# Hybrid encoder layer: moving the bases of the two SBUF stacks from 96 to 0 modulo 128 bytes

## The chip, the cores and the metric

The program runs on one core of one Trainium2 chip, as one launch. The metric is the device time of that launch in microseconds. The kernel before took 2280.51 us, the median of three runs (2278.97, 2280.51 and 2280.64).

## The reference

One encoder layer is applied to two sequences (256 and 1,024 tokens, 1,024 channels, float32) with shared weights. In outline:

```
x = LN(alpha*x + mix(x) @ w_out)      # mix: one input projection, split between
                                      #   a two-way Mamba-2 SSD group (16 heads) and a two-way GLA group (4 heads)
x = LN(alpha*x + cross_attention(x, mem))   # 4 heads, 256 memory tokens a sequence
x = LN(alpha*x + square(relu(x @ w_ff1)) @ w_ff2)   # 4,096 hidden channels
```

All matrices are float32, and the result must keep close to float32 accuracy.

## The kernel before, in words

The 1,280 tokens are ten tiles of 128. Nearly every product is made of three matmuls in the type fp32r: an operand is parted into a rounded part and a remainder (ScalarE copies it into fp32r, VectorE subtracts), and high by high, high by low and low by high are summed in PSUM. A matmul has 512 or 256 columns as a rule and loads its own 128x128 weights. A few products run in plain float32, each as two matmul records, and TensorE also transposes by the identity matrix `ident`.

The work goes in stages: the channel-major input projection with the gates and the convolution (`ch_majors`, L152; `gates`, L365 to L390; `conv`, L463 and L465; `conv_end`, L471; `conv_transposed`, L486 and L487), the token-major projection (`tok_majors`, L167) beside the backward states (L211) and the decay masks, the SSD and GLA passes with the output projection (`project`, L770; `gla_att`, L849), cross-attention (L1024 to L1083), FF1 in a Strassen-like scheme (`prod`, L1222), and FF2 in the same scheme (`mms`, L1445). TensorE's order is written out by hand; SyncE issues nearly all DMAs in program order, each waiting for its own buffers.

What matters here is where tiles lie. SBUF is laid out by two stacks of pools, in bytes of a partition. The **left stack** begins after 1,024 bytes of DMA scratch, four constants of 32 bytes each, `ident` (512), `nhalf` (32) and `gmix` (64): its first further tile, `raw` of the pool `ring`, starts at 1,760, which is 32 modulo 64, 96 modulo 128 and 224 modulo 256. Above it lie the weights `w` of `ring` (9,952) and the stage pools (`p1`, `w5`, `pb`, `mx`, `q2`, `q3`, `pk`, `p4`, `p7`, `pab`, `pa`, `pacc`). The **right stack** grows downwards from 229,344 (96 modulo 128) with `sc`, `io`, `pm`, `px`, `pl` and `pb8`. Sizes are rounded up to 32 bytes, and nearly all of them are multiples of 128, so nearly all tiles of the left stack lie at 96 modulo 128. Right of them, `pm`, `px`, `pl` and `pb8` lie at 96 modulo 128 too, while `io` and parts of `pb` and `q3` lie at 32.

There is one place where residues are mixed. The tag `t5` of the pool `w5` (stage of L152) has eleven buffers of 1,284 floats, 5,136 bytes, which take 5,152: a multiple of 32 and not of 64. So consecutive `t5` buffers start at 0 and at 32 modulo 64 in turn, and all four residues modulo 128 occur. The tiles `xraw`, `gl`, `glg`, `gex`, `cacc`, `csil`, `cxt`, `q` and `k` are such buffers. Of `xraw`, the one for k = 3 starts at 158,304 (32 modulo 64, 96 modulo 256), and the one for k = 4 at 194,368 (0 modulo 64, 64 modulo 256). Two more tiles of `w5` start at 0 modulo 64 (64 modulo 128): `wgk` (143,936) and `lrT` (148,032), the weights and the moving operand of the gates' matmul at L365; and `ident` starts at 1,152, which is 0 modulo 128.

A tile in one stack can take bytes that a closed pool of the other stack held; its first writer then waits for the last reader of those bytes. The tile `X22h` of `pa` ends at 136,928, where `gb3` of `pb8` begins, and `oT` of `p7` ends at 116,448, where the second `hh` buffer of `pb8` begins. `pl` begins at 137,056, which is 128 bytes above the end of `pa`.

Of the kernel before, what the change touches and what calls it, by code (L numbers as in the profile page):

```python
# [8 lines left out]
F32 = mybir.dt.float32  # L9
# [8 lines left out]
P = 128  # L18
# [15 lines left out]
def encoder_layer(ctx: ExitStack, tc: tile.TileContext, A, out, hook=None):  # L34
# [4 lines left out]
    cst = ctx.enter_context(tc.tile_pool(name="cst", bufs=1))  # L39
# [44 lines left out]
        return e.enter_context(tc.tile_pool(name=name, bufs=bufs, reuse_waits="tile", side=side))  # L84

    gmix = cst.tile([P, 16], F32, name="gmix")

    def load_raw(src):
        raw = ring.tile([P, D], F32, tag="raw", name="raw", bufs=2)
        SP.dma_start(raw, src)  # L90
        return raw
# [1501 lines left out]
```

## Time and profile before

| | us |
|---|---|
| median of three runs | 2280.51 |
| lowest and highest run | 2278.97, 2280.64 |
| the profiled execution's own time | 2281.95 |
| its span, first to last instruction | 2280.2 |
| TensorE busy in it | 2243.9 (98%) |
| VectorE, ScalarE, GpSimd busy | 1445.1, 842.5, 353.2 |

The profile is one execution. Its span is what the views divide up; its own time has 1.75 us more around the span. A matmul's record lasts longer than the step from one matmul to the next, since they overlap: the step is the busy time of a long unbroken group divided by its count. The columns of DMA in the view of stretches are the mean share in which the 16 DMA engines were busy and what they moved.

### The profile page before, as it was taken

How to read it: one execution, taken by the hardware profiler on the slowest of the kernel's cores; microseconds unless marked ns; L12 is line 12 of the kernel's file. 1: busy time of each engine (PE TensorE's matmuls, PEld its weight loads, DVE VectorE, ACT ScalarE, POOL GpSimd, SP SyncE). 2: the span in 40 equal slices, each digit the busy share in tenths (PEclk: the TensorE clock that was granted, in tenths of full speed). 3: DMA queues.
4: the chain of work that ended last, by engine and by line, in shares of the span. 5: the costliest groups of instructions: out<-in, count | busy, mean ns of one | idle time of the engine just before them, and what ended most of it. 6: DMA issues, size and time to landing. Idle time of an engine off the chain costs nothing.

```text
span 2280.2 us, 28989 instructions
## 1 busy us (share of the span) xinstructions
PE 2243.9 (98%) x11532; PEld 1910.0 (84%) x11532; DVE 1445.1 (63%) x1760; ACT 842.5 (37%) x1326; POOL 353.2 (15%) x284
## 2 busy tenths in 40 slices
PE   9899999999998999999999999999999999999998
PEld 7788888888877888888888899888888887888887
DVE  5667765578967876898520266585655546675448
ACT  5464332243324324443421333254344434333331
POOL 2114000222223553343000011100000000000002
PEclk9999999999999999999999999999999999999999
DMA  5434326678777556653633432123433349754343
GB/s 177 114 121 129 95 79 218 223 245 275 270 265 267 203 194 245 241 185 130 198 119 85 171 120 83 66 96 128 156 120 135 142 153 332 271 177 139 93 146 140
DMA packets 164637, 384.49 MB, mean 169 GB/s; under 512 B 12899, under 2 KB 67107, under 8 KB 161942
## 3 DMA queue, kind: packets, MB, share of 16 engines
q1 hardware_dynamic: 136310, 363.51, 46.7%
q10 hardware_dynamic: 28192, 19.14, 2.7%
q8 instruction: 90, 1.47, 0.3%
q14 instruction: 45, 0.37, 0.0%
HBM read 262.83 MB, written 119.77 MB: 168 GB/s over the span
## 4 chain that ended last, share of the span: by engine, by line
PE 65%; DVE 3%; DMA 2%; issue 1%; ACT 1%; POOL 0%; POOLq 0%; DVEq 0%; ACTq 0%; SPq 0%
PE ps L1445 16%; PE ps L1222 13%; PE ps L770 8%; PE ps L152 7%; PE ps L1072 5%; PE ps L211 4%; PE ps L1232 4%; PE ps L167 3%; PE ps L1057 2%; DMA raw<-in_w_out 1%; PE ps L702 1%; PE ps L177 1%; PE ps L849 1%; DVE w L112 0%; PE ps L1045 0%
## 5 line engine op out<-in xcount | busy, mean ns | idle before, releaser
L1445 PE MATMUL ps<-w,hh 128*128 128x512 f32 x1608 | 364.9, 389 | 0.6 <-DVE w L1139 0.6
L1445 PEld LDWEIGHTS ps<-w,hh 128*128 128x128 f32 x1608 | 301.8, 188 | 63.6 <-DVE w L1139 1.1
L167 PE MATMUL ps<-w,xh 128*128 128x512 f32 x960 | 299.0, 393 | 2.3 <-DVE w L109 2.3
L152 PE MATMUL ps<-xh,w 128*128 128x512 f32 (+1 forms) x1008 | 232.2, 362 | 7.2 <-ACT k L424 5.3
L770 PE MATMUL ps<-w,mT 128*128 128x512 f32 x960 | 225.4, 393 | 4.5 <-DVE mT L182 2.4
L770 PEld LDWEIGHTS ps<-w,mT 128*128 128x128 f32 x960 | 179.7, 189 | 42.5 <-DVE mT L182 2.8
L167 PEld LDWEIGHTS ps<-w,xh 128*128 128x128 f32 x960 | 179.2, 188 | 39.8 <-DVE w L109 2.7
L152 PEld LDWEIGHTS ps<-xh,w 128*128 128x128 f32 x1008 | 169.1, 190 | 38.4 <-ACT k L424 5.7
L167 PE MATMUL ps<-w,xl 128*128 128x512 f32 x480 | 187.5, 391 | 0.0
L109 DVE TENSOR_TENSOR w<-raw,w 128x1024 fp32r<-128x1024 f32 x65 | 79.3, 1223 | 169.3 <-ACT w L108 169.0
L1362 DVE TENSOR_TENSOR hh<-hr,hh 128x1280 fp32r<-128x1280 f32 (+1 forms) x56 | 80.3, 1434 | 119.9 <-ACT hh L1361 119.9
L1361 ACT ACTIVATE hh<-hr 128x1280 fp32r<-128x1280 f32 (+1 forms) x56 | 68.8, 1228 | 192.4 <-PE ps L1445 180.4
L152 PE MATMUL ps<-xl,w 128*128 128x512 f32 (+1 forms) x504 | 127.5, 361 | 0.0
L1432 POOL TENSOR_SCALAR lnrs<-lnmv 128x1 f32<-128x1 f32 x10 | 5.4, 538 | 758.1 <-DVE lnmv L1430 758.1
L1072 PE MATMUL ps<-w,oT 128*128 128x512 f32 x480 | 110.8, 390 | 0.0
L108 ACT ACTIVATE w<-raw 128x1024 fp32r<-128x1024 f32 x81 | 86.2, 1066 | 63.6 <-PE ps L167 16.1
L671 POOL TENSOR_TENSOR row<-row,cb 128x1024 f32<-128x1024 f32 x20 | 52.8, 2652 | 354.9 <-ACT cb L655 229.2
L167 PEld LDWEIGHTS ps<-w,xl 128*128 128x128 f32 x480 | 90.3, 188 | 19.2
L1139 DVE TENSOR_TENSOR w<-raw,w 128x1024 fp32r<-128x1024 f32 x64 | 70.2, 1100 | 55.3 <-ACT w L1138 55.3
L1072 PEld LDWEIGHTS ps<-w,oT 128*128 128x128 f32 x480 | 89.5, 188 | 18.1
L152 PEld LDWEIGHTS ps<-xl,w 128*128 128x128 f32 x504 | 84.9, 190 | 15.0
L1232 PE MATMUL ps<-x,w 128*128 128x256 f32 x512 | 92.9, 280 | 0.0
(343 smaller groups left out, 4315.4 us busy)
## 6 DMA issues: line engine op xcount, KB each, us to landing
hr<-d_h SPq DMA_DIRECT2D x56, 640.0 KB, 3.9
row<-d_acs SPq DMA_DIRECT2D x40, 512.0 KB, 4.6
d_h<-a SPq DMA_DIRECT2D x16, 1280.0 KB, 4.5
raw<-in_w_ff SPq DMA_DIRECT2D x33, 512.0 KB, 3.5
w<-in_w_ff SPq DMA_DIRECT2D x32, 512.0 KB, 4.8
d_h<-V SPq DMA_DIRECT2D x16, 960.0 KB, 5.5
raw<-in_w_tok SPq DMA_DIRECT2D x28, 512.0 KB, 4.7
raw<-in_w_ch SPq DMA_DIRECT2D x21, 512.0 KB, 3.6
```

The lines of the kernel that those rows point to most:

```text
L108: ACT.activation(w[:, 0], raw, AF.Copy)
L109: eng.tensor_tensor(w[:, 1], raw, f32(w[:, 0]), op=ALU.subtract)
L152: PE.matmul(t[:, :n], wv[:, s, k, :], xx[k][:, o:o + n], start=(k == 0 and i == 0), stop=(k == KD - 1 and i == 2))
L167: PE.matmul(ps, xx[k][:, sl], wv[:, s, k % 2, :], start=(k == 0 and i == 0), stop=(k == KD - 1 and i == 2))
L211: PE.matmul(ps, a[:, p], b[:, q], start=start and i == 0, stop=stop and i == 2)
L770: PE.matmul(ps[j], mT[:, a, k, :], ws[k][:, s, j * 512:(j + 1) * 512], start=(k == 0 and i == 0), stop=(k == KD - 1 and i == 2))
L1072: PE.matmul(ps[j], oT[:, a, k, :], wm[k][:, s, j * 512:(j + 1) * 512], start=(k == 0 and i == 0), stop=(k == KD - 1 and i == 2))
L1139: DVE.tensor_tensor(w[:, 1], raw, f32(w[:, 0]), op=ALU.subtract)
L1222: PE.matmul(ps, wt[:, s, o + k * P:o + (k + 1) * P], xx[:, k, :], start=start and k == 0 and i == 0, stop=stop and k == 3 and i == 2, skip ...
L1232: PE.matmul(ps[:, j * 256:(j + 1) * 256], wt[:, s, o + k % 4 * P:o + (k % 4 + 1) * P], xe[x][:, k, :], start=k == 0 and i == 0, stop=k == ...
L1362: DVE.tensor_tensor(t[:, 1], raw, f32(t[:, 0]), op=ALU.subtract)
L1445: PE.matmul(ps, h[:, a, f, q * P:(q + 1) * P], w[:, b, f * 512:(f + 1) * 512], start=start and i == 0, stop=stop and i == 2, skip_group_ch ...
```

## The change

The pool `cst`, at the base of the left stack, gets a tile of 8 floats (32 bytes) behind `gmix`, and a new pool of one tile of 24 floats (96 bytes) is opened first on the right stack. Nothing reads or writes either tile. The list of instructions stays what it was, with other SBUF addresses: each tile of the left stack behind `gmix` lies 32 bytes higher (`raw` at 1,792 = 14 x 128), each tile of the right stack 96 bytes lower (its top at 229,248 = 1,791 x 128).

```
     gmix = cst.tile([P, 16], F32, name="gmix")
+
+    cst.tile([P, 8], F32, name="left_gap")
+    ctx.enter_context(tc.tile_pool(name="gap", bufs=1, side="right")).tile([P, 24], F32, name="right_gap")
```

## Rows read from the trace of the kernel before

**Rows 1.** From the profile's page: the span, the busy time of the engines, the clock granted to TensorE in 40 slices, and the shares of the chain that ended last.

```profile
span 2280.2 us, 28989 instructions
...
PE 2243.9 (98%) x11532; PEld 1910.0 (84%) x11532; DVE 1445.1 (63%) x1760; ACT 842.5 (37%) x1326; POOL 353.2 (15%) x284
...
PEclk9999999999999999999999999999999999999999
...
PE 65%; DVE 3%; DMA 2%; issue 1%; ACT 1%; POOL 0%; POOLq 0%; DVEq 0%; ACTq 0%; SPq 0%
```

**Rows 2.** The view of stretches, whole stages: start and end in us, its length, busy time and instructions of each engine, granted clock, busy share of the DMA engines and GB/s.

```profile
100.00:300.00 200.00, 200.00 (x1056) 170.03 (x1055) 136.53 (x104) 95.56 (x163) 39.75 (x32) 1.00 0.37 114
300.00:640.00 340.00, 337.43 (x1608) 282.08 (x1607) 242.66 (x291) 111.29 (x175) 66.00 (x26) 0.99 0.66 224
640.00:900.00 260.00, 250.36 (x1313) 211.38 (x1312) 190.00 (x272) 88.08 (x174) 107.19 (x82) 0.99 0.68 233
1890.00:2281.00 391.00, 381.40 (x1682) 315.26 (x1680) 244.32 (x240) 127.91 (x121) 14.91 (x20) 1.00 0.54 183
```

**Rows 3.** What TensorE's matmuls waited for, longest first in total: us, times, longest.

```profile
PE ps L152 <- ACT k L424: 5.3, 1, 5.3
PE ps L211 <- DVE ccp L205: 3.6, 1, 3.6
PE ps L211 <- DVE hl L205: 2.6, 3, 1.9
```

**Rows 4.** TensorE's matmuls in order of time around 136 us: start, length, line, tiles, the shape of the first, and the count. Each of the two rows is one run of 256, 512 and 512 columns.

```profile
135.49 0.75 PE L152 MATMUL ps<-xh,w 128*128 128x256 f32 x3
136.07 0.75 PE L365 MATMUL ps<-lrT,wgk 96*128 96x256 f32 x3
```

**Rows 5.** TensorE's weight loads at the same place, in order of time.

```profile
135.84 0.54 PEld L365 LDWEIGHTS ps<-lrT,wgk 96*128 96x128 f32 x3
136.42 0.54 PEld L152 LDWEIGHTS ps<-xh,w 128*128 128x128 f32 x3
```

**Rows 6.** The views of single lines whose tiles are `t5` buffers at mixed residues: count, shortest, median and longest duration in ns, start of the first and the last.

```profile
L486 PEld LDWEIGHTS ps<-ident,cacc x100: 138/140/146, 230.3 to 353.8; 128*128 128x128 f32 x100
L463 DVE TENSOR_SCALAR cacc<-ub,small x12: 942/945/970, 200.1 to 357.4; 128x1284 f32<-128x1284 f32 x12
L388 DVE SCALAR_TENSOR_TENSOR gex<-gex,k x8: 1479/1484/1487, 89.0 to 204.7; 128x1280 f32<-128x1280 f32 x8
L387 ACT ACTIVATE gex<-glg x16: 1254/1262/1278, 86.3 to 203.1; 128x1280 f32<-128x1280 f32 x16
L471 ACT ACTIVATE csil<-cacc x12: 1277/1314/1322, 214.5 to 366.1; 128x1284 f32<-128x1284 f32 x12
```

**Rows 7.** The view of stretches while the `xraw` tiles for k = 3 (first row) and k = 4 (second row) land; columns as in rows 2.

```profile
10.50:12.00 1.50, 1.50 (x6) 1.21 (x6) 0.97 (x1) 1.26 (x1) 0.00 (x0) 1.00 1.02 423
12.10:13.60 1.50, 1.50 (x6) 1.21 (x5) 1.44 (x1) 1.27 (x1) 0.00 (x0) 1.00 1.01 420
```

**Rows 8.** Groups of matmuls of 128 columns by line: count, busy us, mean ns of one, idle time before. The first has `ident` as the moving operand.

```profile
L486 PE MATMUL ps<-ident,cacc 128*128 128x128 f32 x100 | 12.4, 272 | 0.0
L849 PE MATMUL ps<-qk 128*128 128x128 f32 x160 | 19.5, 275 | 0.0
```

**Rows 9.** Matmuls of L211 in the stretch from 600 to 1060 us, as in rows 6. `gbp` and `qp` lie at the same residue modulo 128 (96), `gfp` (32) and `qp` (96) do not.

```profile
L211 PE MATMUL ps<-gbp,qp x96: 281/285/290, 890.5 to 1049.0; 128*128 128x256 f32 x96
L211 PE MATMUL ps<-gfp,qp x84: 278/279/283, 907.0 to 1048.6; 128*128 128x256 f32 x84
```

**Rows 10.** The matmul groups of FF2, as in rows 8.

```profile
L1445 PE MATMUL ps<-w,hh 128*128 128x512 f32 x1608 | 364.9, 389 | 0.6 <-DVE w L1139 0.6
...
L1445 PE MATMUL ps<-w,he 128*128 128x512 f32 x72 | 16.5, 389 | 0.0
```

**Rows 11.** The instructions that use `X22h` and `oT`, as in rows 6.

```profile
L1222 PE MATMUL ps<-X22h,w x128: 389/389/499, 1509.7 to 1889.9; 128*128 128x512 f32 x128
...
L1072 PE MATMUL ps<-w,oT x480: 389/389/476, 1312.4 to 1487.4; 128*128 128x512 f32 x160
```

**Rows 12.** In order of time: the load of `gb3` on SyncE's queue and the first write of `hh` after FF1's middle.

```profile
1952.85 0.43 SPq L1496 DMA_DIRECT2D gb<-in_ln  x1
...
1880.34 1.28 ACT L1361 ACTIVATE hh<-hr 128x1280 fp32r<-128x1280 f32 x1 [4.02 <-PE ps L1222]
```

## The prediction, made before the changed kernel ran

> **What bounds the kernel now.** [...] What is to be seen is that only 2280.2 - 2243.9 = 36.3 us of the span have no matmul in flight. The stretches [rows 2] say where: 9.6 us between 640 and 900, 9.6 in the last stage (which holds the final normalisation), 2.6 between 300 and 640, none between 100 and 300. TensorE's own waits [rows 3] are single events; the longest is 5.3 us. So two things could move the time: a matmul step that gets shorter or longer, which counts 11,532 times, or the few waits.
>
> **The change, part by part.** It adds no instruction and removes none, so no term of the sum is an instruction. Nor is a step moved past another one, and every queue, SyncE's and GpSimd's among them, keeps its order. What moves is the address of nearly every operand, by 32 bytes up in the left stack and 96 down in the right one. That can act in five ways.
>
> *1. Start of an operand modulo 64, TensorE.* The trace of before already has both cases side by side. At 135.49 us a run of 256, 512 and 512 columns has both operands at 32 modulo 64 (`xh`, `w`); at 136.07 a run of the same shape has both at 0 modulo 64 (`lrT`, `wgk`). Both take 0.75 us [rows 4], and three weight loads take 0.54 us in either [rows 5]. (The second has 96 rows in place of 128; the columns are the same.) Cost of the alignment: 0, within the 0.01 us in which the rows are written.
>
> *2. The same for the other engines.* Lines that work on `t5` buffers hop between 0 and 32 modulo 64 from one instruction to the next. Were the start to matter, each line would show two durations. The weight loads of L486, which meet all four residues modulo 128, go from 138 to 146 ns with the median at 140; VectorE's L463 and L388 have a median within 3 to 5 ns of their shortest; ScalarE's L387 and L471 spread by 24 and 45 ns of some 1,300 [rows 6]. No row gives GpSimd this test; its share of the chain is 0% [rows 1], so that I put it at 0 as well: VectorE and TensorE, which end the chain, are the cover, and if that were gone a few per cent of 353.2 us busy would be the price. Most of these instructions also run beside TensorE's matmuls, so that even the 45 ns would be hidden.
>
> *3. DMA.* The tile for k = 3, at 32 modulo 64, landed while all 16 engines were busy and moved 423 GB/s; the one for k = 4, at 0 modulo 64, 420 [rows 7]. That is 0.7%, and against the aligned one. DMA is 2% of the chain, 45.6 us, so the bound is 0.3 us to either side; I take 0. [...]
>
> *4. A start at 0 modulo 128, TensorE.* Here the trace of before has no fp32r matmul. The nearest rows are of 128 columns: the transposes move `ident`, which lies at 0 modulo 128, and last 272 ns; the plain products of L849 move operands at 32 modulo 128 and last 275 [rows 8]. If the 3 ns were the address, 11,532 of them are 34.6 us. The other end is a loss of the same 3 ns, for which no row speaks. I take 0: the two groups differ in kind as well (a transpose is one record of its own kind, a plain product two), and the weight loads in rows 6 did not care for 0 modulo 128. [...]
>
> *5. The stacks come 128 bytes closer.* Within a stack all distances stay. Between them they shift by 128, so in FF2 `w` (9,952) and `hh` (116,448), whose distance is now a multiple of 256, will be 128 off. For an effect of distance the nearest rows are L211's: with the same residue (`gbp`, `qp`) the median is 285 ns, with another (`gfp`, `qp`) 279 [rows 9]. FF2 has 1,608 + 72 = 1,680 such matmuls [rows 10]; at 6 ns that is 10.1 us, up or down, since which distance is the better is open. I take 0, because FF2's step of 364.9 us / 1,608 = 227 ns shows no room where the operands wait for each other.
>
> Closer stacks also make new overlaps in time. `gb3` now takes the last 128 bytes of `X22h`, so its load must wait for that tile's last reader, and on SyncE's queue the loads of `hr` and `w` would stand behind it, and TensorE behind those. But `X22h` is last read at 1889.9 us [rows 11] and the load goes out at 1952.85 [rows 12]: 63 us of slack, so 0. The second `hh` buffer now overlaps `oT`, last read by a matmul that begins at 1487.4 [rows 11], while `hh` is written from 1880.3 on [rows 12]: 0 too. The gap of 128 bytes below `pl` is used up exactly, so the tiles still fit.
>
> The sum is 0. Against the profiled execution, whose own time is 2281.95 us, that is 2281.95; the median of the runs shown is 1.44 lower, and for a median I predict **2280.5 us**.
>
> **The rivals.**
>
> *Faster: the fp32r matmul gains from 0 modulo 128.* Price 3 ns a matmul, 34.6 us, 2246. For it: rows 8. Against it: rows 4 and 6, in which halfway to that alignment, and for weight loads all the way, nothing changed. Chance 0.06.
>
> *Slower: the distance between the stacks.* The place is FF2, where `w` and `hh` lie in different stacks, the price 6 ns for each of 1,680 matmuls, 10.1 us, 2290.6. It decides if a distance that is an odd multiple of 128 is the bad one for two operands read at once. For it: in rows 9 the distance goes with 6 ns. Against it: there the equal residue is the slower one, and the two groups also stand at other places of their sequences. Chance 0.05.
>
> [...]
>
> *The change does not reach what it says.* In `io`, a tile goes from 32 to 64 modulo 128, and the `t5` buffers only swap residues. This holds whatever the effect is, and would shrink any of the above; the time stays at 2280.5.
>
> **How the numbers follow.** A measurement of this kernel can tell about 0.2%, 4.6 us, from no change. No change, with the 0.3 us of DMA and the 2.4 below it, has 0.87; the gain at 0 modulo 128 has 0.06, to which 0.01 comes for the distance turning out better (2270.4); the loss by distance 0.05, and 0.01 for a loss at 0 modulo 128. So faster 0.07, same 0.87, slower 0.06. As the case "same" holds more than 8 in 10 alone, the range is its own: below, 2280.5 - 2.4 and the 1.5 us by which the lowest run lies under the median, rounded to 2277; above, the same 3.5 us, 2284.
>
> **What would show it.** Right: FF2's group again at 227 ns a step, the 256-512-512 run at L152 again at 0.75 us, L463 at 945 ns and busy sums of all engines within 0.2%. The faster rival would show at once in L1445 and L167, records of 386 ns or less in place of 389, and a TensorE busy time near 2,210 us. The slower one would show in L1445 alone, with L167 and L770 unchanged. [...] The prediction is wrong if the median leaves 2277 to 2284, whichever step does it.

## The result, and the profile after

The changed kernel is slower: median 2299.74 us (four runs, 2296.55 to 2303.68) against 2280.57 (2278.97 to 2282.47), a ratio of 1.0088 with the interval 1.0076 to 1.0101, 17 to 23 us. The forecast of 2280.5 and its range of 2277 to 2284 are wrong. In the code after, every line behind the edit has a number higher by 3: L1445 is L1448.

The page of the changed kernel, its parts 1, 2 and 4, answers to [rows 1]. The profiled execution's own time is 2297.25 us.

```profile
span 2295.5 us, 28989 instructions
...
PE 2260.1 (98%) x11532; PEld 1910.1 (83%) x11532; DVE 1445.3 (63%) x1760; ACT 841.8 (37%) x1326; POOL 351.3 (15%) x284
...
PEclk9999999999999999999999999999999999999999
...
PE 66%; DVE 3%; DMA 2%; issue 1%; ACT 1%; POOL 1%; POOLq 0%; DVEq 0%; ACTq 0%; SPq 0%
```

The span grew by 15.3 us and TensorE's busy time by 16.2, while its weight loads, VectorE, ScalarE and GpSimd are where they were, within 2 us, and the clock is at the top digit everywhere (0.996 in the mean of either execution). So no wait was added (35.4 us of the span have no matmul in flight, where it was 36.3): matmuls became longer. Which ones is read from the groups of matmuls, parted by shape: line, engine, operation, tiles, shapes, count, busy us, mean ns of one record. First those of the kernel before that [rows 10] does not have:

```profile
L167 PE MATMUL ps<-w,xh 128*128 128x512 f32 x960 | 299.0, 393 | 2.3 <-DVE w L109 2.3
L770 PE MATMUL ps<-w,mT 128*128 128x512 f32 x960 | 225.4, 393 | 4.5 <-DVE mT L182 2.4 <-ACT w L111 1.6 <-DVE w L112 0.6
...
L1232 PE MATMUL ps<-x,w 128*128 128x256 f32 x512 | 92.9, 280 | 0.0
L1222 PE MATMUL ps<-X,w 128*128 128x512 f32 x384 | 91.7, 389 | 0.0
...
L1232 PE MATMUL ps<-x89l,w 128*128 128x256 f32 x256 | 72.2, 282 | 0.0
...
L1222 PE MATMUL ps<-KT,w 128*128 128x512 f32 x192 | 46.1, 389 | 0.0
L1222 PE MATMUL ps<-S4h,w 128*128 128x512 f32 x128 | 42.5, 393 | 1.5 <-DVE a L1298 1.5
L1222 PE MATMUL ps<-X22h,w 128*128 128x512 f32 x128 | 42.3, 391 | 1.7 <-DVE a L1297 1.7
...
L1222 PE MATMUL ps<-S1h,w 128*128 128x512 f32 x128 | 42.0, 389 | 0.0
L152 PE MATMUL ps<-mh,w 128*128 128x512 f32 x128 | 41.1, 393 | 0.0
...
L167 PE MATMUL ps<-w,mh 128*128 128x512 f32 x128 | 40.0, 394 | 0.0
```

and the same groups of the changed kernel:

```profile
L1448 PE MATMUL ps<-w,hh 128*128 128x512 f32 x1608 | 374.1, 395 | 0.5 <-DVE w L1142 0.5
L170 PE MATMUL ps<-w,xh 128*128 128x512 f32 x960 | 299.1, 392 | 2.1 <-DVE w L112 2.1
...
L773 PE MATMUL ps<-w,mT 128*128 128x512 f32 x960 | 224.8, 393 | 4.7 <-DVE mT L185 2.4 <-ACT w L114 1.8 <-DVE w L115 0.6
...
L1235 PE MATMUL ps<-x,w 128*128 128x256 f32 x512 | 94.6, 283 | 0.0
L1225 PE MATMUL ps<-X,w 128*128 128x512 f32 x384 | 93.9, 394 | 0.0
...
L1235 PE MATMUL ps<-x89l,w 128*128 128x256 f32 x256 | 72.5, 283 | 0.0
...
L1225 PE MATMUL ps<-KT,w 128*128 128x512 f32 x192 | 46.8, 392 | 0.0
L1225 PE MATMUL ps<-S4h,w 128*128 128x512 f32 x128 | 42.8, 395 | 1.5 <-DVE a L1301 1.5
L1225 PE MATMUL ps<-X22h,w 128*128 128x512 f32 x128 | 42.8, 395 | 1.6 <-DVE a L1300 1.6
...
L1225 PE MATMUL ps<-S1h,w 128*128 128x512 f32 x128 | 41.9, 388 | 0.0
L155 PE MATMUL ps<-mh,w 128*128 128x512 f32 x128 | 41.8, 399 | 0.0
L170 PE MATMUL ps<-w,mh 128*128 128x512 f32 x128 | 40.6, 398 | 0.0
...
L1225 PE MATMUL ps<-S1l,w 128*128 128x512 f32 x64 | 25.3, 395 | 0.0
...
L1448 PE MATMUL ps<-w,he 128*128 128x512 f32 x72 | 16.9, 395 | 0.0
```

FF2's group went from 364.9 us [rows 10] to 374.1, a step of 364.9/1,608 = 226.9 ns to one of 232.6; its record from 389 to 395 ns. What is to be seen is which groups did *not* move. The large groups whose operands both lie in the left stack (`w` with `xh` and, of the same kind, `mT`) are the same. Those that lengthened have one operand in each stack (`w` with `hh` and `he`; `X` with `w`; `w` with `mh`), or stand in a sequence with such matmuls (`KT`, and `X22h`, which alternates with the remainder `X22l` in the right stack).

The sum: FF2 9.2 + 0.4 us; FF1 at 512 columns 2.2 (`X`) + 0.7 (`KT`) + 0.3 (`S4h`) - 0.1 (`S1h`) + 0.4 (`S1l`, 24.9 before) + 1.6 for four further groups of L1225 of the same kind, 5.1 in all; L1235 1.7 + 0.3; the products with `mh` 0.7 + 0.6, and with its remainder `ml` 0.7. That is 18.7 us, near the 19.2 between the medians. The busy time of the two profiled executions differs by 2.5 less: L155's groups with `xh` and `xl` came out 3.0 us lower in this one, and some smaller groups a few tenths to either side. The operands of L155 keep their distance, and its largest group, 208.2 us before and 206.3 here, comes out at anything between 206.4 and 208.3 in the kernels below whose left stack lies as before; so I read that as the difference of one execution from another.

### The profile page after: what moved, and what is told of

The parts are those of the page before. It is cut to its first block, busy times and chain, and to the rows that moved or that the text cites. A ratio compares the mean times of both kernels' runs of the same rounds, so it can differ in the third digit from the quotient of the medians.

```text
span 2295.5 us, 28989 instructions
## 1 busy us (share of the span) xinstructions
PE 2260.1 (98%) x11532; PEld 1910.1 (83%) x11532; DVE 1445.3 (63%) x1760; ACT 841.8 (37%) x1326; POOL 351.3 (15%) x284
## 4 chain that ended last, share of the span: by engine, by line
PE 66%; DVE 3%; DMA 2%; issue 1%; ACT 1%; POOL 1%; POOLq 0%; DVEq 0%; ACTq 0%; SPq 0%
PE ps L1448 17%; PE ps L1225 12%; PE ps L773 8%; PE ps L155 7%; PE ps L1075 4%; PE ps L214 4%; PE ps L1235 4%; PE ps L170 4%; PE ps L1060 1%; PE ps L705 1%; DMA raw<-in_w_out 1%; PE ps L180 1%; PE ps L852 1%; DVE w L115 0%; PE ps L1048 0%
## 5 line engine op out<-in xcount | busy, mean ns | idle before, releaser
L1448 PE MATMUL ps<-w,hh 128*128 128x512 f32 x1608 | 374.1, 395 | 0.5 <-DVE w L1142 0.5
L1448 PEld LDWEIGHTS ps<-w,hh 128*128 128x128 f32 x1608 | 302.9, 188 | 71.5 <-DVE w L1142 0.9
L155 PE MATMUL ps<-xh,w 128*128 128x512 f32 (+1 forms) x1008 | 230.2, 360 | 6.4 <-ACT k L427 5.3
L155 PEld LDWEIGHTS ps<-xh,w 128*128 128x128 f32 x1008 | 167.4, 189 | 37.5 <-ACT k L427 5.6
L155 PE MATMUL ps<-xl,w 128*128 128x512 f32 (+1 forms) x504 | 127.0, 359 | 0.8 <-DVE xl L258 0.6
L111 ACT ACTIVATE w<-raw 128x1024 fp32r<-128x1024 f32 x81 | 86.1, 1066 | 64.9 <-PE ps L170 16.2
L170 PEld LDWEIGHTS ps<-w,xl 128*128 128x128 f32 x480 | 90.2, 188 | 19.2
L155 PEld LDWEIGHTS ps<-xl,w 128*128 128x128 f32 x504 | 83.9, 189 | 16.6 <-DVE xl L258 1.9
L1235 PE MATMUL ps<-x,w 128*128 128x256 f32 x512 | 94.6, 283 | 0.0
```

The lines of the kernel that those rows point to most:

```text
L111: ACT.activation(w[:, 0], raw, AF.Copy)
L155: PE.matmul(t[:, :n], wv[:, s, k, :], xx[k][:, o:o + n], start=(k == 0 and i == 0), stop=(k == KD - 1 and i == 2))
L170: PE.matmul(ps, xx[k][:, sl], wv[:, s, k % 2, :], start=(k == 0 and i == 0), stop=(k == KD - 1 and i == 2))
L1235: PE.matmul(ps[:, j * 256:(j + 1) * 256], wt[:, s, o + k % 4 * P:o + (k % 4 + 1) * P], xe[x][:, k, :], start=k == 0 and i == 0, stop=k == ...
L1448: PE.matmul(ps, h[:, a, f, q * P:(q + 1) * P], w[:, b, f * 512:(f + 1) * 512], start=start and i == 0, stop=stop and i == 2, skip_group_ch ...
```

## The experiments

Two theories stood. **The distance** (called D): the two operands of a matmul, the moving one and the weights, are read by TensorE in ways that depend on how far apart they lie modulo 256 bytes; the change took pairs across the stacks from 0 to 128 apart. **The alignment**: a start at 0 modulo 128, or at 0 modulo 256, is bad for an fp32r operand by itself. They were told apart by moving both stacks together, each alone, and then single tiles. Distances below are weights minus moving operand, modulo 256; counted the other way round, as in some expectations, 224 is 32 and 160 is 96. In FF2 `hh` holds the weights and the tile named `w` moves.

### Both stacks down by 96: starts change, distances don't

```
-    nhalf = cst.tile([P, 1], F32, name="nhalf")
+    lowp = ctx.enter_context(tc.tile_pool(name="low", bufs=1, side="right"))
+    nhalf = lowp.tile([P, 1], F32, name="nhalf")
...
-    gmix = cst.tile([P, 16], F32, name="gmix")
+    gmix = lowp.tile([P, 16], F32, name="gmix")
```

The two small constants lie at the base of the right stack instead, so that both stacks begin 96 bytes lower, on multiples of 128 as in the changed kernel (`raw` at 128 modulo 256).

> Both stacks 96 bytes lower (the 96 bytes of nhalf and gmix go to the base of the right stack): every base is a multiple of 128, as in the changed kernel, but all distances stay as before. Theory D (the distance between the weights in the left stack and the other operand in the right one sets the step): no change, 2280 +- 3 us, L1445 at 227 ns a step. Rival A (an operand that starts on 128 modulo 256 is slow): at least as slow as the changed kernel, 2300 us or more, with L1445 at 232 or more, and L167 and L770 slow too, since now both stacks start there.

Measured: 2281.27 us (ten runs), ratio to the kernel before 0.9998, 0.9987 to 1.0008. Its groups of matmuls:

```profile
L1446 PE MATMUL ps<-w,hh 128*128 128x512 f32 x1608 | 365.0, 389 | 0.6 <-DVE w L1140 0.6
...
L1223 PE MATMUL ps<-S4h,w 128*128 128x512 f32 x128 | 42.5, 392 | 1.5 <-DVE a L1299 1.5
L1223 PE MATMUL ps<-S1h,w 128*128 128x512 f32 x128 | 42.0, 389 | 0.0
```

(The kernel before had a median of 2281.50 us beside it.) With both bases on 128 the step is back at 227 ns: a start on a multiple of 128 costs and gives nothing here. What this kernel does not try is a start at 0 modulo 256, where the left stack of the changed kernel lies; the next kernels do.

### One stack alone

Three kernels, each the kernel before with one unused tile.

```
+    ctx.enter_context(tc.tile_pool(name="gap", bufs=1, side="right")).tile([P, 32], F32, name="right_gap")   # right128
+    ctx.enter_context(tc.tile_pool(name="gap", bufs=1, side="right")).tile([P, 24], F32, name="right_gap")   # right96
+    cst.tile([P, 8], F32, name="left_gap")                                                                   # left32
```

> Only a gap of 128 bytes at the base of the right stack: the distance is that of the changed kernel, and no base is a multiple of 128 (224 and 96 modulo 256). Theory D: as slow as the changed kernel, 2300 +- 4 us, L1445 at 232 ns a step. Rival A: 2280 us, 227 ns.

> The other half: the right stack 96 bytes lower, on 128 modulo 256; the left one as before. Distance 96 off. Theory D: between 2285 and 2300, L1445 between 228 and 232 ns. Rival A: all of the loss, 2300, since it is the right stack that lies on 128 modulo 256.

> One half of the change: the left stack 32 bytes higher, a multiple of 256; the right one as before. Distance 32 off. Theory D gives no size for 32: if it counts by 128 there is no change, 2280; if it grows evenly, a quarter of the loss, 2285. Rival A: the right stack is not on 128, 2280. A loss here of more than half, 2290, would speak for the left base by itself.

The kernel before had a median of 2281.50 us beside these three.

| kernel | FF2's distance | median, us | ratio to before |
|---|---|---|---|
| right stack -128 | 128 | 2299.15 | 1.0083 (1.0068 to 1.0098) |
| right stack -96 | 160 | 2301.55 | 1.0096 (1.0081 to 1.0111) |
| left stack +32 | 224 | 2299.96 | 1.0089 (1.0072 to 1.0106) |

Groups of matmuls with the right stack 128 lower (all starts keep 32 modulo 64, so no alignment changes):

```profile
L1446 PE MATMUL ps<-w,hh 128*128 128x512 f32 x1608 | 374.1, 395 | 0.4 <-DVE w L1140 0.4
```

with the right stack 96 lower:

```profile
L1446 PE MATMUL ps<-w,hh 128*128 128x512 f32 x1608 | 375.6, 395 | 0.4 <-DVE w L1140 0.4
...
L1223 PE MATMUL ps<-S1h,w 128*128 128x512 f32 x128 | 42.7, 394 | 0.0
```

and with the left stack 32 higher:

```profile
L1446 PE MATMUL ps<-w,hh 128*128 128x512 f32 x1608 | 375.6, 395 | 0.4 <-DVE w L1140 0.4
...
L1223 PE MATMUL ps<-S1h,w 128*128 128x512 f32 x128 | 42.4, 393 | 0.0
```

The first makes the changed kernel's time, and its 374.1 us, without putting any base on a multiple of 128; this and the experiment before it show that the distance between the stacks is the cause, and the alignment falls as an explanation. The last was a miss: I had expected little of a shift by 32, and it costs as much as any. By what was expected of it, such a loss would speak for the left base by itself, which lies at 0 modulo 256 there; but the first kernel leaves that base where it was and loses the same. The second, too, came out just above the 2285 to 2300 us and 228 to 232 ns that were expected. So 128 is not a special bad distance; 0 is the special good one. `S1h` shows a second thing. Its own distance stays 0 in these two kernels, yet its record goes from 389 to 393 and 394. It alternates with matmuls that move `S1l`, which did shift: a neighbour in the sequence takes part.

### FF2's `hh` alone put back

```
     gb3 = [pb.tile([P, 2, D], F32, name="gb3")]
+    pb.tile([P, 32], F32, name="pad8")
```

This is the changed kernel with 128 bytes more in FF2's pool, which puts `hh` back at 0 apart from `w` and leaves everything else as changed, FF2's 72 matmuls with `he` too.

> The changed kernel with a pad of 128 bytes in pb8 alone: FF2's right-hand tiles come back to a distance of 0 modulo 256 from the weights, all else stays changed. Theory D: L1445 back at 227 ns, 9 us of the 19 given back, 2291. If instead the loss in FF2 comes from somewhere else (another engine's traffic, absolute starts), L1445 stays at 232 ns and the time at 2300.

Measured: 2289.36 us (five runs), ratio to the kernel before 1.0038, 1.0024 to 1.0053. Its groups:

```profile
L1449 PE MATMUL ps<-w,hh 128*128 128x512 f32 x1608 | 365.0, 389 | 0.6 <-DVE w L1142 0.6
...
L1225 PE MATMUL ps<-X,w 128*128 128x512 f32 x384 | 93.9, 394 | 0.0
...
L170 PE MATMUL ps<-w,mh 128*128 128x512 f32 x128 | 40.6, 398 | 0.0
L1449 PE MATMUL ps<-w,he 128*128 128x512 f32 x72 | 16.9, 395 | 0.0
```

FF2's 9.1 us come back, the groups with `X`, `mh` and `he` keep the loss, and 1.0088 - 1.0038 = 0.0050 of 2280.5, 11 us, is what `hh` had cost by the medians, some 4 us to either side by the two intervals. By the traces, 9.1 of the 18.7 us above, about half of the loss is its.

### FF2's buffers at other distances

The kernel before, with each of the three `hh` buffers longer by an unused piece, so that the buffers lie at three distances; everything outside FF2 is untouched.

```
+    def hh_new():
+        t = pb.tile([P, 2576], F32R, tag="hh", name="hh", bufs=3)   # 2560 + 16; the others + 8, + 8, + 32
+        return t[:, 0:2560].rearrange("p (s f l) -> p s f l", s=2, f=2)
...
-    hh0 = [pb.tile([P, 2, 2, 640], F32R, tag="hh", name="hh", bufs=3)]
+    hh0 = [hh_new()]
...
-        return pb.tile([P, 2, 2, 640], F32R, tag="hh", name="hh", bufs=3)[:, :, :, :n]
+        return hh_new()[:, :, :, :n]
```

The second kernel with +8 has 128 bytes of `pad8` as well.

> The kernel before, with each of the three hh buffers 64 bytes larger, so that they lie 64, 128 and 192 off the weights modulo 256; nothing else of TensorE's operands moves. Theory D, as the halves of the change left it (any distance but 0 is slow): each buffer at 230 to 234 ns a step. If the distance counts modulo 128 or 64, the buffer at 128, or all three, are at 227.

> The same with 32 bytes more a buffer: 160, 192 and 224 off. Theory D: each at 230 to 234 ns a step, L1445 9 us longer in sum. If only distances of up to 128 above the weights matter, all three stay at 227.

> The same 128 bytes lower: 32, 64 and 96 off. Theory D: each at 230 to 234 ns a step. A step below 226 at any distance would mean that a better distance than the one of before exists, worth 1,680 times the difference in FF2.

> The kernel before, with each of the three hh buffers 128 bytes larger, so that they lie 128, 256 and 384 lower than a multiple of 256 would put them all: distances 128, 0 and 128 modulo 256. One execution, one stage, one list of instructions, and the buffers take turns. Theory D: the middle buffer at 227 ns a step, the two others at 232 to 233, L1445 in sum two thirds of the loss of the changed kernel, 6 us above 364.9. Against D: one step for all three.

| buffers longer by | distances | own time of one run, us | FF2's group, us | its step, ns |
|---|---|---|---|---|
| 64 bytes | 64, 128, 192 | 2292.46 | 375.3 | 233.4 |
| 32 bytes | 160, 192, 224 | 2288.25 | 375.6 | 233.6 |
| 32 bytes, and the pad | 32, 64, 96 | 2290.33 | 376.0 | 233.8 |
| 128 bytes | 128, 0, 128 | 2287.18 | 371.5 | 231.0 |

The kernels before beside them had a median of 2279.65 us (the first three) and 2280.29 (the last). The group of each, in this order, first 64 bytes:

```profile
L1449 PE MATMUL ps<-w,hh 128*128 128x512 f32 x1608 | 375.3, 395 | 0.4 <-DVE w L1139 0.4
```

32 bytes:

```profile
L1449 PE MATMUL ps<-w,hh 128*128 128x512 f32 x1608 | 375.6, 396 | 0.4 <-DVE w L1139 0.4
```

32 bytes and the pad:

```profile
L1450 PE MATMUL ps<-w,hh 128*128 128x512 f32 x1608 | 376.0, 396 | 0.4 <-DVE w L1139 0.4
```

128 bytes, the whole group and then three stretches within FF2 (2001 to 2007, 2007.9 to 2013.9 and 1994 to 2000.5 us), each of which lies within the matmuls on one buffer:

```profile
L1449 PE MATMUL ps<-w,hh 128*128 128x512 f32 x1608 | 371.5, 393 | 0.5 <-DVE w L1139 0.5
...
L1449 PE MATMUL ps<-w,hh 128*128 128x512 f32 x27 | 6.4, 395 | 0.0
...
L1449 PE MATMUL ps<-w,hh 128*128 128x512 f32 x29 | 6.7, 389 | 0.0
...
L1449 PE MATMUL ps<-w,hh 128*128 128x512 f32 x29 | 6.9, 395 | 0.0
```

Seven distances other than 0 were met, and each costs 6 to 7 ns a step. Parted by buffer, the starts of the records give a mean step of 232.4 to 233.0 ns at 128 and of 233.1 to 234.1 at each of the six others; 128 is the mildest, by up to 1 ns. The last kernel has both cases in one execution: on the buffer at 0 the record is 389 ns, on the two buffers before it 395, with the same instructions, at a mean granted clock of 0.995 for the execution. The buffer at 0 lies 256 bytes lower than before, so that it is the distance modulo 256 that counts, and not modulo 512. Two thirds of the difference of 9.2 us on 364.9 would be 371.0; it is 371.5.

### Can the kernel before be made faster this way?

In the kernel before nearly all pairs are 0 apart, which is the good case. The exceptions and the matmuls of 256 columns were left. There [rows 9] had 6 ns the other way: 285 at 0 apart, 279 at another distance. So one kernel put `S4h` from 128 to 0 apart, and the products of 256 columns that use `qp` with `KT`, and `x1h`, 64 away from 0.

```
+    p4.tile([P, 16], F32, name="pad4")
...
+    p7.tile([P, 16], F32, name="pad7", bufs=1)
...
+    p7.tile([P, 48], F32, name="pad7b", bufs=1)
...
+    pl.tile([P, 32], F32, name="padl")
```

> Three places where the traces leave something to gain, each in a stage of its own, in the kernel before: gb2 and with it S4h 128 bytes lower (distance 128 to 0), the tile qp of p7 64 bytes higher (256-column matmuls, distance 0 to 64), and x1h and x1l 64 bytes higher (runs of 256 and 512 columns, distance 0 to 64). Theory D: S4h from a mean record of 393 ns to 389, worth 0.5 us; qp's matmuls 2 ns a step faster as gfp's are, 0.4 us; x1's 512-column steps up from 231 to 233 and the 256-column ones down, about nothing. In all 2279.5, which a measurement can't tell from no change.

Measured: 2279.45 us (ten runs) against 2280.29, ratio 0.9997, 0.9987 to 1.0006: no gain that can be told. Its groups:

```profile
L152 PE MATMUL ps<-x1h,w 128*128 128x512 f32 x256 | 78.1, 397 | 0.0
...
L1226 PE MATMUL ps<-S4h,w 128*128 128x512 f32 x128 | 42.2, 390 | 1.5 <-DVE a L1302 1.5
...
L152 PE MATMUL ps<-x1h,w 128*128 128x256 f32 x128 | 35.8, 280 | 0.0
...
L211 PE MATMUL ps<-KT,qp 128*128 128x256 f32 x192 | 24.6, 284 | 0.0
```

Every group moved as the distance says: `S4h` from 393 to 390 ns; `KT` with `qp` from 25.0 us and 286 ns to 24.6 and 284; `x1h` from 286 to 280 ns at 256 columns (36.5 us before) and, at 512 columns, from 394 to 397 (77.9 us before). The gains and the loss add up to 0.3 + 0.4 + 0.7 - 0.2 = 1.2 us, less than a measurement can tell; in the same execution two groups whose tiles were not moved came out longer than before by 2.0 us (`w` with `mT`) and 0.9 (`x` with `mt`). The time stays with the kernel before.

## Why the prediction was wrong

**The failed step is part 5, the distance between the stacks, which was put at 0.** The effect was named there, with FF2 as the place and 6 ns as the price: FF2 lost 9.2 + 0.4 us where the 6 ns gave 10.1 (that they fit so well is luck, as the rows behind them show below). What failed is the sentence that took 0, "because FF2's step of 364.9 us / 1,608 = 227 ns shows no room where the operands wait for each other". That this step has no room was an estimate; no run shows the shortest step that is possible. Even where it holds, it speaks against a gain and says nothing against a loss. The kernel before was at the good end already, and the runs show 232.6 to 233.8 at every other distance tried. The rival that this step fed got 0.05.

**The rival itself was too small.** It priced FF2 alone, 2290.6. FF1 (7.1 us with L1235) and the products with `mh` and `ml` (2.0) also have operands in both stacks, and I did not go through the groups by the stacks of their tiles. With them the sum would have been near 2299. Its sign "L1445 alone, with L167 and L770 unchanged" held for `xh` and `mT` and not for `mh` and FF1.

**Its condition was wrong too.** "An odd multiple of 128" is not what decides: 32, 64, 96, 160, 192 and 224 cost as much as 128, or up to a nanosecond more (233.1 to 234.1 ns a step in FF2, where 128 has 232.4 to 233.0).

**Rows 9 were the wrong rows for it.** They are of 256 columns, and at that length the sign is the opposite: there 0 is the slow distance, as `KT` with `qp` (286 ns at 0, 284 at 64) and `x1h` (286 at 0, 280 at 192) confirm, and L1235 too: there the change brought `x89l` from 128 to 0 apart, and its record went from 282 to 283 ns, that of its neighbour `x` from 280 to 283. The right rows stood in the trace of before, unread: `S4h` (in the pool `pl`, at 96 modulo 256, with weights at 224) is 128 apart and shows 393 ns, `S1h`, of the same line, shape and count, is 0 apart and shows 389. The experiment that put `S4h` at 0 apart brought it to 390. That was a price of 4 ns a matmul, with its sign, in the right length.

**Right were the other steps.** Part 1 and part 4, the start modulo 64 and 128: both stacks on multiples of 128 left the time at 0.9998, so the faster rival (2246) is gone. Part 2, the other engines: three of the lines of [rows 6] in the changed kernel, each with its own view (count, shortest, median, longest in ns):

```profile
L489 PEld LDWEIGHTS ps<-ident,cacc x100: 137/140/146, 228.1 to 351.5; 128*128 128x128 f32 x100
...
L466 DVE TENSOR_SCALAR cacc<-ub,small x12: 941/944/3124, 198.2 to 355.1; 128x1284 f32<-128x1284 f32 x12
...
L390 ACT ACTIVATE gex<-glg x16: 1253/1258/1277, 84.2 to 201.1; 128x1280 f32<-128x1280 f32 x16
```

The medians are within 4 ns of before (the one instruction of 3,124 ns on L466 is a single one of twelve). Part 3, DMA: the tiles `raw` now start on 256, and the page's medians from issue to landing are 3.5 us for `in_w_ff` and 3.6 for `in_w_ch`, as before. The 2.4 us by which the prediction's range and its case "same" reach below no change are a term that no run shows; what the runs showed in its place is these two landings unchanged, and a share of DMA in the chain of 2% in both traces. The new overlaps cost nothing: TensorE's longest waits are 5.3 us (L427) and 3.1 (L208), where [rows 3] had 5.3 and 3.6.

**What stays open.** What makes the steps longer, no run shows. If it is two reads that meet, which is a guess, it is open which: a matmul's moving operand with its own weights, or with the weights that are loaded for the next one while it runs (in FF2 the record of that load starts 2 to 4 ns after the matmul's own and lasts 187 to 192). In nearly all matmuls both have the same distance, and no run was made to part them; but the traces have places where they differ. In the kernel with buffers longer by 128 bytes, the last matmul on the buffer at 0 runs while the first weights of a buffer at 128 are loaded. The last of these five is such a one:

```profile
L1449 PE MATMUL ps<-w,hh x5: 389/389/396, 2013.2 to 2014.1; 128*128 128x512 f32 x5
```

From its start to the next there are 232 ns, where the matmuls before it have 227, and so it is at all 18 such places (232 or 233). Between `S1h` and `S1l` of the changed kernel, where the moving operand goes from 0 to 128 apart and the weights stay where they are, it is the step of `S1l` itself that is longer, 234 ns, and not that of `S1h` before it, 227. Both speak for the weights that are loaded meanwhile, without proving it.

How far the influence of a neighbour reaches can be read too. In the changed kernel `KT`, 0 apart all through, stands behind matmuls at 128 in FF1, and in the sequence below its first nine matmuls of twelve have a median of 395 ns (first row) and its last three the 389 of before (second row). The other sequences of `KT` behind `X` take three to ten to come back, most of them nine.

```profile
L1225 PE MATMUL ps<-KT,w x9: 387/395/398, 1695.7 to 1697.5; 128*128 128x512 f32 x9
...
L1225 PE MATMUL ps<-KT,w x3: 389/389/389, 1697.8 to 1698.2; 128*128 128x512 f32 x3
```

`S1h` follows there, and beside `S1l` at 128 it keeps its 388. `X22h` has the same distances, but as a rule comes right behind `X` at 128, and shows 395; `S4h` comes behind it and shows 395 as well, although the change brought it to 0 apart. So what went before a sequence counts, and not only its own distances. Why a lengthening lasts so long, and why `S1h` loses 4 to 5 ns where `S1l` is 96 or 32 apart and none where it is 128, the runs do not show.

## What to carry to other kernels

An edit that adds no instruction can still shift one stack of tiles against the other, so ask of every group of matmuls where both of its operands lie and what their distance becomes; in this kernel fp32r matmuls of 512 columns want 0 modulo 256 (227 ns a step in FF2, against 232.6 to 233.8). Before an effect is put at 0, look in the trace for two groups of the same line and shape that differ in it (`S4h` and `S1h` here), not for a pair of another shape. And a step that seems to have no room to get shorter can get longer, as here from 227 ns to 233: argue the two ends of a range separately.

## What was unexpected of the hardware

The step of an fp32r matmul of 512 columns is 227 ns when its weights and its moving operand are 0 apart modulo 256 bytes and 232.6 to 233.8 at 32, 64, 96, 128, 160, 192 and 224 apart, at a granted clock of 0.99 to 1.00. At 256 columns it is the other way round: a group's record is longer at 0 apart, by 6 ns (`x1h`, against 192), 2 ns (`KT` with `qp`, against 64) and 1 ns (`x89l`, against 128). Moving both stacks together by 96 bytes changed nothing (0.9998). And the lengthening outlasts the matmuls at another distance: `KT`, at 0 apart, took nine matmuls behind them to get back to 389 ns.
